# Last modulation block of the FFN summed on VectorE, four column blocks summed over half of the rows first, second norm from three means, three resident loads

## The chip, the cores and the metric

The program runs on one core of one Trainium2 chip. The metric is the device time of one execution in microseconds (us). Engines are named as in the profile: PE (TensorE, matrix products), DVE (VectorE), ACT (ScalarE), POOL (GpSimd) and SP (SyncE, which here issues the loads). SBUF is the on-chip memory, PSUM holds what PE writes (a PSUM tile is called a bank). "Landing" is the time from the issue of a load until its data is there.

## The reference, cut to what matters

A decoder layer on 256 rows of 2048 numbers. All numbers are float32.

```python
mod = silu(c) @ w_ada + b_ada                      # 2048 -> 6 x 2048
shift_a, scale_a, gate_a, shift_f, scale_f, gate_f = split(mod, 6)
h = rms_norm(x, g_attn_pre) * (1 + scale_a) + shift_a
proj = h @ w_in                                    # then attention of two kinds
mixed = concat([diff_out, dsa_out]) @ w_o
x = x + gate_a * rms_norm(mixed, g_attn_post)
h = rms_norm(x, g_ffn_pre) * (1 + scale_f) + shift_f
ff = (silu(h @ w_gate) * (h @ w_up)) @ w_down      # inner width 5632
x = x + gate_f * rms_norm(ff, g_ffn_post)
```

## The kernel before

**Tiles.** The 256 rows are two tiles t of 128 rows. The inner dimension of 2048 is 16 steps k of 128. A weight block of 4 k by 512 columns is 1 MB: `wload` (L159) loads it into `raw` (L163, a ring of six), and splits it into a high part `whi` (a copy on ACT, L179) and the rest `wlo` (a subtraction on DVE, L180), 1024 columns at a time, in rings of three. Each product of a k, a t and 512 columns is three matmuls (`mm3`, L192 high by high, L195 high by rest, L196 rest by high), so a block of 1 MB is 24 matmuls of 128x512.

**Stages.** `w_in` in groups of k; attention, mixed with the last group and with columns 0 to 1023 of `w_o`; columns 1024 to 2047 of `w_o` (two column blocks, ci = 2 and 3); the residual and the second norm; the transposed input of the FFN; the FFN in three groups of 4, 4 and 3 column blocks of 512, each gate, up and down.

**Modulation.** The vector `mod` is summed beside all this, in units of 1 MB of `w_ada` (L223), which share the ring of six. `ada_block` (L203) makes a unit either on PE, as four matmuls of 32x512 into the bank `ad` (L236; each shows as two rows of the trace), with an eviction at the end (L253), or on DVE, as four `scalar_tensor_tensor` of 128x512 into an accumulator `aacc` (L244). Shift and scale of the FFN (`modF`) are made in four blocks, 0 to 3, of 512 columns of each: 8 units, which are 64 rows of L236 on PE, or 32 instructions on DVE. When a block is summed, a few small matmuls and two DVE instructions put it into `modF`: L293 where it was on PE, L297 where it was on DVE. Block 2 is made on DVE (`F_DVE`, L41), the others on PE. Block b is needed for the steps k = 4b to 4b + 3 of the FFN's input. `side()` and the loops call `ada_step` to use some units after each weight block.

**Tail of `w_o`.** `tail_pair` (L786) runs the column blocks 2 and 3 for both t together, but keeps the last two weight blocks resident, and runs them first for t = 0, then for t = 1: 24 matmuls each, pinned in this order. After those of t = 0 comes `residual(0)`, which thus lies beside 24 matmuls of t = 1. The same function ends the program with `w_down`.

**Residual and second norm.** `post` (L773) squares a bank on ACT with a running sum (L783) and multiplies it by the gate on DVE (`y`, L784). `residual` (L852) sums the squares, takes the power −1/2 on POOL (`ry`, L156), adds y · ry to `x1` on DVE (two instructions, L859), squares the new x1 on ACT (two, L861), and on POOL adds (L862), scales (L155), takes the power (L156) and fills the diagonal matrix `dg[t]` (L864). The FFN's input `H2` is made by `h2_tiles` (L842): matmuls of x1 by `dg[t]` (L846, which transpose and norm), then shift and scale and the split into a high and a low half (`make_h`, L348, L350, L345, L347), first for k = 0 to 7, later for 8 to 15.

**First halves.** To start before blocks 2 and 3 of `modF` are there, the first `NSPLIT` column blocks of gate and up are summed over k = 0 to 7 and put aside in `part` (an ACT copy); the second half is added later on DVE (L925).

**Order.** A scheduler orders the instructions of all engines ahead of time; `keep_in_program_order` pins some. Each engine runs its queue in order, so an instruction that waits holds all behind it.

## Time and profile before

| | us |
|---|---|
| median of 3 runs (lowest to highest) | 1262.45 (1262.14 to 1264.23) |
| the profiled execution | 1263.92 |
| its span in the trace | 1262.1 |
| PE busy | 1230.5 (97%) |
| DVE busy | 763.6 (60%) |
| ACT busy | 573.1 (45%) |
| POOL busy | 23.2 (2%) |
| mean granted TensorE clock | 0.997 |

The span runs from the first to the last instruction of the trace; 1.8 us of the profiled execution lie outside it. A row of the timeline gives start, length, engine, source line, tiles (`out<-in`) and, in brackets, how long the engine was idle ahead of it and what released it. The lengths of matmuls overlap: one starts 0.2265 us after the other, though each is listed with 0.39. Rows with "x3" merge several instructions.

### The profile page before, as it was taken

The numbers are of one execution on the slowest core, as the hardware profiler recorded it, in microseconds if no ns is written. First come the engines' busy times: TensorE is split into PE (matmuls) and PEld (weight loads), VectorE is DVE, ScalarE is ACT, GpSimd is POOL, SyncE is SP. The second block draws the span as 40 slices with busy tenths as digits, with TensorE's granted clock in tenths as the row PEclk, the third lists the DMA queues.
The fourth block names the chain that finished last, engine by engine and source line by source line (L and its number), as shares of the span: only waits on it lengthen the run. The fifth ranks groups of instructions, "written<-read, shape, count | busy, mean of one in ns | idle before, by whom it ended". The sixth has DMA issues, their size and how long they took to land.

```text
span 1262.1 us, 15223 instructions
## 1 busy us (share of the span) xinstructions
PE 1230.5 (97%) x5912; PEld 948.6 (75%) x5912; DVE 763.6 (60%) x1155; ACT 573.1 (45%) x838; POOL 23.2 (2%) x63
## 2 busy tenths in 40 slices
...
GB/s 382 388 358 334 371 357 204 370 258 272 200 304 266 150 366 279 267 190 322 314 278 262 179 192 241 255 172 195 199 177 192 200 191 185 193 198 182 185 134 67
DMA packets 44713, 310.14 MB, mean 246 GB/s; under 512 B 5848, under 2 KB 5848, under 8 KB 7648
## 3 DMA queue, kind: packets, MB, share of 16 engines
...
q8 instruction: 46, 0.75, 0.2%
...
q10 hardware_dynamic: 272, 0.00, 0.0%
HBM read 307.05 MB, written 2.10 MB: 245 GB/s over the span
## 4 chain that ended last, share of the span: by engine, by line
PE 93%; DMA 2%; ACT 2%; DVE 1%; issue 1%; POOL 0%; SPq 0%; DVEq 0%; POOLq 0%
PE mm L195 27%; PE mm L192 27%; PE mm L196 27%; PE ad L236 5%; DMA raw<-in_w_ada_dram 1%; PE tr L490 1%; DMA raw<-in_w_in_dram 1%; PE tr L429 1%; PE tr L934 1%; PE tr L410 1%; PE tr L846 1%; PE tr L312 1%; DVE wlo L180 0%; PE tr L293 0%; PE tr L513 0%
## 5 line engine op out<-in xcount | busy, mean ns | idle before, releaser
L180 DVE TENSOR_TENSOR wlo<-raw,whi 128x1024 fp32r<-128x1024 f32 (+1 forms) x383 | 463.4, 1213 | 369.0 <-ACT whi L179 368.2
L179 ACT ACTIVATE whi<-raw 128x1024 fp32r<-128x1024 f32 (+1 forms) x383 | 401.0, 1051 | 519.5 <-PE mm L196 488.6
L195 PE MATMUL mm<-wlo,h 128*128 128x512 f32 (+1 forms) x1056 | 415.1, 393 | 0.8 <-DVE wlo L180 0.8
L196 PE MATMUL mm<-whi,h 128*128 128x512 f32 (+1 forms) x1056 | 410.9, 389 | 1.6 <-DVE h L350 1.6
L192 PE MATMUL mm<-whi,h 128*128 128x512 f32 (+1 forms) x1056 | 380.1, 393 | 1.9 <-ACT whi L179 1.0
L192 PEld LDWEIGHTS mm<-whi,h 128*128 128x128 f32 x1056 | 196.7, 188 | 63.3 <-issue 13.4
L195 PEld LDWEIGHTS mm<-wlo,h 128*128 128x128 f32 x1056 | 198.6, 188 | 60.3 <-issue 10.8
L196 PEld LDWEIGHTS mm<-whi,h 128*128 128x128 f32 x1056 | 198.6, 188 | 42.3 <-DVE h L350 2.1
L195 PE MATMUL mm<-wlo,gT 128*128 128x512 f32 x348 | 135.8, 390 | 0.0
L196 PE MATMUL mm<-whi,gT 128*128 128x512 f32 x348 | 135.4, 389 | 0.0
L192 PE MATMUL mm<-whi,gT 128*128 128x512 f32 x348 | 123.0, 390 | 0.0
L244 DVE SCALAR_TENSOR_TENSOR aacc<-raw,csil,aacc 128x512 f32<-128x512 f32 x126 | 94.0, 747 | 8.0 <-DMA raw<-in_w_ada_dram 5.3
L236 PE MATMUL ad<-raw,c 128*32 128x512 f32 (+2 forms) x640 | 82.8, 523 | 12.8 <-DMA raw<-in_w_ada_dram 12.8
L748 DVE TENSOR_TENSOR PR<-mm,PR 128x512 f32<-128x512 f32 (+1 forms) x88 | 57.0, 669 | 34.2 <-PE mm L196 34.0
L196 PEld LDWEIGHTS mm<-whi,gT 128*128 128x128 f32 x348 | 65.3, 188 | 13.9 <-issue 0.2
L195 PEld LDWEIGHTS mm<-wlo,gT 128*128 128x128 f32 x348 | 65.3, 188 | 13.6 <-issue 0.2
L192 PEld LDWEIGHTS mm<-whi,gT 128*128 128x128 f32 x348 | 65.3, 188 | 13.5
L195 PE MATMUL mm<-wlo,mixT 128*128 128x512 f32 x124 | 49.9, 402 | 0.0
L236 PEld LDWEIGHTS ad<-raw,c 128*32 128x32 f32 x640 | 17.9, 111 | 41.6 <-issue 26.7
L192 PE MATMUL mm<-whi,mixT 128*128 128x512 f32 x124 | 47.6, 402 | 0.7 <-ACT mixT L603 0.7
L196 PE MATMUL mm<-whi,mixT 128*128 128x512 f32 x124 | 45.9, 394 | 0.0
L195 PEld LDWEIGHTS mm<-wlo,mixT 128*128 128x128 f32 x124 | 23.3, 188 | 8.4 <-issue 1.7
(192 smaller groups left out, 673.2 us busy)
## 6 DMA issues: line engine op xcount, KB each, us to landing
...
```

Source lines behind the costliest of these rows:

```text
L179: made = [ACT.activation(hv, src, AF.Copy), DVE.tensor_tensor(lv, src, hv.bitcast(F32), op=ALU.subtract)]
L180: DVE.tensor_tensor(lv, src, hv.bitcast(F32), op=ALU.subtract)]
L192: i = PE.matmul(ps, lhsT=hi, rhs=whi, start=start, stop=False)
L195: PE.matmul(ps, lhsT=hi, rhs=wlo, start=False, stop=False)
L196: PE.matmul(ps, lhsT=lo, rhs=whi, start=False, stop=stop)
L236: PE.matmul(st["ps"][32 * j:32 * j + 32, :n], lhsT=c33[:, k, 1 - b:33 - b], rhs=w, start=(b == 0 and k < 4), stop=(b == nb - 1 and k >= 12 ...
L244: DVE.scalar_tensor_tensor(acc, w, csil[:, k:k + 1], acc, op0=ALU.mult, op1=ALU.add)
L312: PE.matmul(ps, lhsT=ones, rhs=accs[0], start=True, stop=True)
L410: PE.transpose(tr[:, i * P:(i + 1) * P], PR[:, t, c0:c0 + P], ident)
L429: PE.matmul(sc[i][:, SEG[t]], lhsT=st["q"][r, (2 * j + t) * P:(2 * j + t + 1) * P], rhs=ikT[r, :P * (t + 1)], start=True, stop=True)
L490: PE.matmul(sc[i][:, SEG[t]], lhsT=l, rhs=r, start=True, stop=True)
L748: DVE.tensor_tensor(dst, banks[c0][t][:, :n], dst, op=ALU.add)
```

## The change

- `F_DVE` is (2, 3): block 3 of `modF` is summed on DVE too. `FRATE` is 1: one unit instead of two after each half block of the first halves. `side()` in the tail stops two units into block 2 (`SIDE`).
- `NSPLIT` is 4: four column blocks are summed over k = 0 to 7 first. Their partial sums lie in `part`, in the buffer of `Ga` and in the tiles `xhi` and `xlo`. The load of `Gf` (the gate of the FFN), which shares the buffer of `Ga`, and its units come later, ahead of the fourth column block.
- `tail_pair` keeps the last three weight blocks resident: 36 pinned matmuls for each t. The first stays in the rings of `whi` and `wlo`, the second half in the rings and half in `xhi` and `xlo`, the third in the part of `H2` for k = 8 to 15, which is free then.
- The second norm doesn't square the new x1. With m1 the mean of the squared bank, m2 twice the mean of y · x1 and m3 the mean of y squared, ry = (m1 + eps)^(−1/2), and the mean square of the new x1 is m3 · ry² + m2 · ry + the mean square of x. `post_attn` makes the three sums by column block: two squares on ACT, y and a product with a running sum (`tensor_tensor_reduce`, L801) on DVE. `residual` then has a reduce, two small DVE steps, and three steps on POOL (`ry`, `r1`, `dg`); the updates of x1 come behind.
- `h2_tiles` works on pairs of k: shift and scale of one on DVE and of one on ACT, then one copy and one subtraction for both.

```diff
-F_DVE = (2,)
+F_DVE = (2, 3)
-FRATE = 2
+FRATE = 1
-NSPLIT = 2
+NSPLIT = 4
+SIDE = 2
...
     def tail_pair(rows, L, kbase, nk, cs, banks, side, done):
 
-        blocks = [(a, ci) for a in range(0, nk - 4, 4) for ci in cs]
-        for a, ci in blocks:
+        blocks = [(a, ci) for a in range(0, nk, 4) for ci in cs]
+        for a, ci in blocks[:-3]:
...
-        tl = {ci: wload(rows, kbase + nk - 4, 4, ci * 512, 512, ph2 if ci == cs[1] else None)
-              for ci in cs}
+
+        spare = [tuple(ph2.tile([P, 1024], F32R, tag=tag, name=nm(tag)) for tag in ("xhi", "xlo"))]
+        spare += [tuple(H2[:, i, k:k + 4, :].rearrange("p k q -> p (k q)") for i in range(2)) for k in (8, 12)]
+        homes = (None, (None, spare[0]), spare[1:])
+        tl = [(ci, wload(rows, kbase + a, 4, ci * 512, 512, homes[i])) for i, (a, ci) in enumerate(blocks[-3:])]
         for t in range(T):
-            for ci in cs:
-                for (k, _), (whi, wlo) in tl[ci].items():
+            for ci, ws in tl:
+                for (k, _), (whi, wlo) in ws.items():
...
     def side():
-        ada_step(1)
+        if used[0] < need_f1 + SIDE:
+            ada_step(1)
...
+    def post_attn(bank, t, ci):
+
+
+        cs_ = slice(ci * 512, ci * 512 + 512)
+        j = tr_bank()
+        ACT.activation(j, bank, AF.Square, scale=D ** -0.5, accum_out=st3[:, t, 0, ci:ci + 1])
+        DVE.tensor_tensor(y[:, t, cs_], bank, Ga[:, cs_], op=ALU.mult)
+        j2 = ph2.tile([P, 512], F32, tag="sil", name=nm("j2"), bufs=3)
+        DVE.tensor_tensor_reduce(out=j2, in0=y[:, t, cs_], in1=x1[:, t, cs_], scale=2.0 / D, scalar=0.0,
+                                 op0=ALU.mult, op1=ALU.add, accum_out=st3[:, t, 1, ci:ci + 1])
+        ACT.activation(j, y[:, t, cs_], AF.Square, scale=D ** -0.5, accum_out=st3[:, t, 2, ci:ci + 1])
...
     def residual(t):
+
         for ci in (2, 3):
-            post(banks[ci, t], t, ci, Ga, ssy, y)
-        DVE.tensor_reduce(sst[:, t:t + 1], ssy[:, t], axis=AX.X, op=ALU.add)
-        rstd(ry[:, t:t + 1], sst[:, t:t + 1], 1, D)
+            post_attn(banks[ci, t], t, ci)
+        DVE.tensor_reduce(mean[:, t], st3[:, t], axis=AX.X, op=ALU.add)
+        rt = ry[:, t:t + 1]
+        POOL.tensor_tensor(rt, mean[:, t, 0:1], nhalf[:, 0:1], op=ALU.pow)
+        m = mean[:, t, 1:2]
+        DVE.scalar_tensor_tensor(m, mean[:, t, 2:3], rt, m, op0=ALU.mult, op1=ALU.add)
+        tc.keep_in_program_order(
+            DVE.scalar_tensor_tensor(m, m, rt, msx[:, t:t + 1], op0=ALU.mult, op1=ALU.add))
+        POOL.tensor_tensor(r1[:, t:t + 1], m, nhalf[:, 0:1], op=ALU.pow)
+        POOL.tensor_scalar(dg[t], ident, r1[:, t:t + 1], None, op0=ALU.mult)
         for h in range(2):
             hs = slice(1024 * h, 1024 * h + 1024)
-            DVE.scalar_tensor_tensor(x1[:, t, hs], y[:, t, hs], ry[:, t:t + 1], x1[:, t, hs],
-                                     op0=ALU.mult, op1=ALU.add)
-            ACT.activation(y[:, t, hs], x1[:, t, hs], AF.Square, accum_out=ss1[:, t, h:h + 1])
-        POOL.tensor_tensor(sss[:, t:t + 1], ss1[:, t, 0:1], ss1[:, t, 1:2], op=ALU.add)
-        rstd(r1[:, t:t + 1], sss[:, t:t + 1], 1, D, POOL)
-        POOL.tensor_scalar(dg[t], ident, r1[:, t:t + 1], None, op0=ALU.mult)
+            tc.keep_in_program_order(
+                DVE.scalar_tensor_tensor(x1[:, t, hs], y[:, t, hs], rt, x1[:, t, hs], op0=ALU.mult, op1=ALU.add))
...
-    Gf = big.tile([P, D], F32, tag="Ga", name="Gf")
-    tc.keep_in_program_order(SP.dma_start(Gf, g_ffn_post[0].partition_broadcast(P)))
...
-            for b in range(4):
-                ada_gate(Gf, 5, b * 512, False)
         for lc in range(ng):
+            if fc == NSPLIT - 1:
+                Gf = big.tile([P, D], F32, tag="Ga", name="Gf")
+                tc.keep_in_program_order(SP.dma_start(Gf, g_ffn_post[0].partition_broadcast(P)))
+                for b in range(4):
+                    ada_gate(Gf, 5, b * 512, False)
```

The scheduler orders the changed program anew; up to the start of columns 1024 to 2047 of `w_o` (about 452 us of the trace) the order is as it was. Three places follow. Names carry the numbers of the program, so that `dg0` is of t = 0 and `dg1` of t = 1.

PE at the end of the tail, before: the last resident matmuls of t = 1, four units of block 3 (`ad826`), the transposes by `dg0`, and the first gate matmul.

```order
L195 MATMUL mm788_3876<-xlo837_4147,mixT286_1559 128x512
L196 MATMUL mm788_3876<-xhi836_4146,mixT287_1560 128x512
L236 MATMUL ad826_4123<-raw875_4366,c33_105 32x512 x4
L236 MATMUL ad826_4123<-raw876_4372,c33_105 32x512 x4
L236 MATMUL ad826_4123<-raw882_4412,c33_105 32x512 x4
L236 MATMUL ad826_4123<-raw883_4418,c33_105 32x512 x4
L846 MATMUL tr846_4236<-dg0_3871,x1_3850 128x128 x4
L846 MATMUL tr851_4257<-dg0_3871,x1_3850 128x128 x4
L192 MATMUL mm868_4326<-whi871_4330,h2_3866 128x512
```

The same place of PE in the changed program:

```order
L193 MATMUL mm791_3885<-h2_3876,mixT286_1564 128x512
L196 MATMUL mm791_3885<-h2_3876,mixT286_1564 128x512
L197 MATMUL mm791_3885<-h2_3876,mixT287_1565 128x512
L870 MATMUL tr836_4194<-dg0_3880,x1_3848 128x128 x4
L870 MATMUL tr839_4209<-dg0_3880,x1_3848 128x128 x4
L193 MATMUL mm850_4261<-whi853_4265,h2_3876 128x512
L196 MATMUL mm850_4261<-wlo854_4266,h2_3876 128x512
L197 MATMUL mm850_4261<-whi853_4265,h2_3876 128x512
L193 MATMUL mm850_4261<-whi853_4265,h2_3876 128x512
```

The units of block 3 are gone from PE, here and in the tail ahead; the transposes by `dg0` stand right behind the resident matmuls. Those by `dg1` stand behind 14 matmuls of `mm850`, and the third of these (L197) is the first that reads the low half of h2.

DVE at the residual of t = 0, before: the two `y` of t = 0, the sum and its scaling, the x1 updates, then the first `wlo` of the FFN and a `y` of t = 1.

```order
L784 TENSOR_TENSOR y_3853<-mm785_3873,Ga_142 128x512
L784 TENSOR_TENSOR y_3853<-mm787_3875,Ga_142 128x512
L855 TENSOR_REDUCE sst_3867<-ssy_3316 128x1
L155 TENSOR_SCALAR rs840_4181<-sst_3867 128x1
L859 SCALAR_TENSOR_TENSOR x1_3850<-y_3853,ry_3317,x1_3850 128x1024 x2
L180 TENSOR_TENSOR wlo872_4331<-raw870_4328,whi871_4330 128x1024
L784 TENSOR_TENSOR y_3853<-mm786_3874,Ga_142 128x512
```

The same place of DVE in the changed program, from the second `y` of t = 0; `raw872` is the last unit of block 2, `mm790` the last bank of t = 0:

```order
L245 SCALAR_TENSOR_TENSOR aacc871_4381<-raw872_4386,csil_103,aacc871_4381 128x512
L799 TENSOR_TENSOR y_3851<-mm790_3884,Ga_147 128x512
L245 SCALAR_TENSOR_TENSOR aacc871_4381<-raw872_4386,csil_103,aacc871_4381 128x512
L801 ISA j2831_4127,st3_119<-y_3851,x1_3848 128x512
L801 ISA st3_119 128x1
L181 TENSOR_TENSOR wlo854_4266<-raw852_4263,whi853_4265 128x1024
L890 TENSOR_REDUCE mean_3878<-st3_119 128x3
L181 TENSOR_TENSOR wlo856_4270<-raw852_4263,whi855_4269 128x1024
L894 SCALAR_TENSOR_TENSOR mean_3878<-mean_3878,ry_3321 128x1
L181 TENSOR_TENSOR wlo860_4306<-raw858_4303,whi859_4305 128x1024
L896 SCALAR_TENSOR_TENSOR mean_3878<-mean_3878,ry_3321,msx_117 128x1
L902 SCALAR_TENSOR_TENSOR x1_3848<-y_3851,ry_3321,x1_3848 128x1024 x2
```

Three `wlo` of the FFN's first blocks and the last sums of block 2 now stand in front of and between the steps of the residual. The first `y` of t = 0 and its product sum (L801) stand just ahead, each again between sums of `raw872`.

DVE in the first FFN blocks, before: `wlo`, and the shift, scale and split of h2.

```order
L180 TENSOR_TENSOR wlo888_4427<-raw886_4424,whi887_4426 128x1024
L348 TENSOR_SCALAR hf925_4672<-tr922_4659,modF_109 128x128
L350 TENSOR_TENSOR h2_3866<-hf924_4668,h2_3866 128x128
L350 TENSOR_TENSOR h2_3866<-hf925_4672,h2_3866 128x128
L180 TENSOR_TENSOR wlo890_4431<-raw886_4424,whi889_4430 128x1024
L348 TENSOR_SCALAR hf928_4685<-tr927_4680,modF_109 128x128
```

DVE at that stage of the changed program; `raw892` and `raw902` are units of block 3:

```order
L245 SCALAR_TENSOR_TENSOR aacc901_4561<-raw892_4510,csil_103,aacc901_4561 128x512
L181 TENSOR_TENSOR wlo877_4395<-raw873_4388,whi876_4394 128x1024
L245 SCALAR_TENSOR_TENSOR aacc901_4561<-raw892_4510,csil_103,aacc901_4561 128x512
L181 TENSOR_TENSOR wlo883_4435<-raw881_4432,whi882_4434 128x1024
L245 SCALAR_TENSOR_TENSOR aacc901_4561<-raw892_4510,csil_103,aacc901_4561 128x512 x2
L181 TENSOR_TENSOR wlo885_4439<-raw881_4432,whi884_4438 128x1024
L245 SCALAR_TENSOR_TENSOR aacc901_4561<-raw902_4566,csil_103,aacc901_4561 128x512 x2
L181 TENSOR_TENSOR wlo889_4475<-raw887_4472,whi888_4474 128x1024
L245 SCALAR_TENSOR_TENSOR aacc901_4561<-raw902_4566,csil_103,aacc901_4561 128x512
```

Between the `wlo` there are now the sums of block 3, four to each unit of 1 MB; where a unit's load is awaited, the next `wlo` waits behind it.

## Rows read from the trace of the kernel before

**Rows 1.** The page of the profile, part 1 (busy time, share of the span, instructions of each engine) and part 4 (the chain of work that ended last, by engine).

```profile
PE 1230.5 (97%) x5912; PEld 948.6 (75%) x5912; DVE 763.6 (60%) x1155; ACT 573.1 (45%) x838; POOL 23.2 (2%) x63
...
PE 93%; DMA 2%; ACT 2%; DVE 1%; issue 1%; POOL 0%; SPq 0%; DVEq 0%; POOLq 0%
```

**Rows 2.** Busy time in stretches of 20 us around the end of the attention part and in the FFN; columns: stretch, its length, busy us (and instructions) of PE, PEld, DVE, ACT and POOL, granted TensorE clock, share of the DMA engines, GB/s.

```profile
500.00:520.00 20.00, 16.13 (x95) 10.97 (x95) 13.90 (x25) 13.98 (x32) 5.42 (x11) 0.91 0.92 375
...
580.00:600.00 20.00, 20.00 (x94) 16.66 (x93) 19.51 (x25) 8.71 (x11) 0.00 (x0) 1.00 0.88 319
```

**Rows 3.** PE's instructions in order of time in the last part of `w_o`; columns: start us, us, engine, line, operation, tiles, number of instructions in the row.

```profile
463.06 0.39 PE L196 MATMUL mm<-whi,mixT 128*128 128x512 f32 x1
463.38 1.06 PE L236 MATMUL ad<-raw,c 128*32 128x512 f32 x8
...
464.71 0.39 PE L196 MATMUL mm<-whi,mixT 128*128 128x512 f32 x1
...
470.05 1.05 PE L236 MATMUL ad<-raw,c 128*32 128x512 f32 x2
...
490.40 1.06 PE L236 MATMUL ad<-raw,c 128*32 128x512 f32 x8
...
492.43 0.39 PE L196 MATMUL mm<-whi,mixT 128*128 128x512 f32 x1
492.75 1.07 PE L236 MATMUL ad<-raw,c 128*32 128x512 f32 x8
...
494.18 1.06 PE L236 MATMUL ad<-raw,c 128*32 128x512 f32 x6
...
495.51 0.39 PE L196 MATMUL mm<-whi,mixT 128*128 128x512 f32 x1
```

**Rows 4.** PE in order of time from the end of the tail into the first FFN block; same columns, and in brackets the idle time ahead of the row and what ended it.

```profile
497.78 0.39 PE L192 MATMUL mm<-whi,mixT 128*128 128x512 f32 x1
...
502.99 0.39 PE L196 MATMUL mm<-xhi,mixT 128*128 128x512 f32 x1
503.31 3.64 PE L236 MATMUL ad<-raw,c 128*32 128x512 f32 x32
508.25 2.05 PE L846 MATMUL tr<-dg,x 128*128 128x128 f32 x16 [1.30 <-POOL dg L864]
...
512.41 0.50 PE L196 MATMUL mm<-whi,h 128*128 128x512 f32 x1 [1.65 <-DVE h L350]
513.84 0.79 PE L192 MATMUL mm<-whi,h 128*128 128x512 f32 x1 [0.93 <-ACT h L345]
514.43 0.63 PE L195 MATMUL mm<-wlo,h 128*128 128x512 f32 x1
...
516.56 2.16 PE L846 MATMUL tr<-dg,x 128*128 128x128 f32 x16
```

**Rows 5.** DVE in order of time across the residual of the first 128 rows.

```profile
498.70 0.69 DVE L784 TENSOR_TENSOR y<-mm,Ga 128x512 f32<-128x512 f32 x1 [4.43 <-ACT tr L783]
499.30 0.15 DVE L855 TENSOR_REDUCE sst<-ssy 128x1 f32<-128x4 f32 x1
...
500.30 2.48 DVE L859 SCALAR_TENSOR_TENSOR x<-y,ry,x 128x1024 f32<-128x1024 f32 x2 [0.66 <-POOL ry L156]
...
504.44 2.35 DVE L180 TENSOR_TENSOR wlo<-raw,whi 128x1024 fp32r<-128x1024 f32 x2
```

**Rows 6.** POOL in order of time: two of the attention part, then the residuals of both halves of the rows.

```profile
256.88 0.70 POOL L156 TENSOR_TENSOR rsd<-rs,nhalf 128x2 f32<-128x2 f32 x1 [4.73 <-DVE rs L155]
...
270.87 1.12 POOL L156 TENSOR_TENSOR rsd<-rs,nhalf 128x2 f32<-128x2 f32 x1 [13.00 <-DVE rs L155]
...
505.80 1.04 POOL L155 TENSOR_SCALAR rs<-sss 128x1 f32<-128x1 f32 x1
506.92 0.56 POOL L156 TENSOR_TENSOR r<-rs,nhalf 128x1 f32<-128x1 f32 x1
507.58 0.62 POOL L864 TENSOR_SCALAR dg<-ident,r 128x128 f32<-128x128 f32 x1
...
513.26 0.19 POOL L155 TENSOR_SCALAR rs<-sss 128x1 f32<-128x1 f32 x1
```

**Rows 7.** DVE in order of time beside POOL's instruction at 270.87.

```profile
270.69 1.53 DVE L244 SCALAR_TENSOR_TENSOR aacc<-raw,csil,aacc 128x512 f32<-128x512 f32 x2
```

**Rows 8.** DVE's groups by line and shape over the whole span; columns: line, operation, tiles, shapes, number, busy us, mean ns of one, idle time ahead and what ended it.

```profile
L180 DVE TENSOR_TENSOR wlo<-raw,whi 128x1024 fp32r<-128x1024 f32 x374 | 456.5, 1224 | 365.4 <-ACT whi L179 364.7
L244 DVE SCALAR_TENSOR_TENSOR aacc<-raw,csil,aacc 128x512 f32<-128x512 f32 x126 | 94.0, 747 | 8.0 <-DMA raw<-in_w_ada_dram 5.3 <-DMA aacc<-in_b_ada_dram 1.6
...
L501 DVE CUSTOM_DVE_ANT_0 s<-tr,mask 128x256 f32<-128x256 f32 x16 | 6.7, 418 | 0.0
...
L501 DVE DVE_READ_ACCUMULATOR2_ANT mx<- 128x1 f32 x48 | 3.9, 82 | 0.0
```

**Rows 9.** From issue to landing of the 1 MB loads issued from 440 to 560 us: first those of `w_ada` (L223), then those of the weights (L163).

```profile
DMA to landing us min/median/max: 4.7/5.8/8.2
...
DMA to landing us min/median/max: 4.8/6.9/12.6
```

**Rows 10.** The last matmul of the program on PE, and DVE's sum of its result.

```profile
1252.63 0.39 PE L196 MATMUL mm<-xhi,gT 128*128 128x512 f32 x1
...
1253.39 0.68 DVE L780 TENSOR_TENSOR ff<-mm,ff 128x512 f32<-128x512 f32 x1
```

More of the change, by code (lines that the diff above doesn't have):

```diff
@@ L169, in wload @@
                 w = min(step, n - b)
-                if more is not None and a + m == nk:
-                    hi = more.tile([P, 1024], F32R, tag="xhi", name=nm("xhi"))
-                    lo = more.tile([P, 1024], F32R, tag="xlo", name=nm("xlo"))
+                home = more[a // 2] if more else None
+                if home is not None:
+                    hi, lo = home
                 else:
@@ L322, in layer @@
     rstd(rx, ssx, T, D)
+    msx = ct([P, T], "msx")
+    DVE.tensor_scalar(msx, ssx, 1.0 / D, EPS, op0=ALU.mult, op1=ALU.add)
+    st3 = ct([P, T, 3, 5], "st3")
+    POOL.memset(st3, 0.0)
+    POOL.memset(st3[:, :, 0, 4:5], EPS)
     def x_tiles(k0):
```

38 lines of the change are left out of this document (27 added, 11 removed).

## The prediction

> **What bounds the kernel now.** I read the page first. PE is busy 97% of the span and is 93% of the chain that ended last [rows 1]; the granted clock is 1.00 but for a few us. So a change pays only if it takes instructions off PE, or shortens one of PE's few waits. Next I read the timeline of PE where the change lies, from the last part of `w_o` into the first FFN block. Two things stand there. First, `ad` matmuls (L236), which sum block 3 of the FFN's shift and scale on PE: small clusters between the weight matmuls [rows 3], and 32 rows in a burst of 3.64 us [rows 4]. Second, the only waits of this region: 1.30 us for `dg`, 1.65 and 0.93 us for the first half of h2, and then a stretch at the low clock (mean 0.91 from 500 to 520 us [rows 2]). One weight matmul costs (502.99 − 497.78) / 23 = 0.2265 us at full clock [rows 4]; the five from 514.43 to 516.56 take 2.13 us where 1.13 would do, and the one at 513.84 takes 0.59 where some 0.3 would do, so the low clock cost 1.3 us. Waits and low clock together: 1.30 + 1.65 + 0.93 + 1.3 = 5.2 us.
>
> The profiled execution took 1263.92 us, 1.47 above the median; I sum against it and take 1.47 off at the end.
>
> **The `ad` matmuls go.** The cluster at 463.38 stands between matmuls that start at 463.06 and 464.71; two steps of 0.2265 would end at 463.51, so it costs 1.20 us [rows 3]. The two at 492.75 and 494.18 stretch the three steps from 492.43 (to 493.11) to 495.51: 2.40 us. With those at 470.05 and 490.40 at 1.2 each, the clusters cost 6.0 us; even the one of two rows at 470.05 lasts 1.05 us. The burst costs 3.64. Together **−9.64 us**. The finish of the blocks is even: block 2's eight L297 were spread out and block 3's L293 stood in one piece; now block 2's stand in one piece and block 3's are spread.
>
> **What takes their place.** Block 3 is 32 `scalar_tensor_tensor` on DVE, of 0.75 us each [rows 8], about 24 us, between the `wlo` of the first FFN blocks. Per 24 matmuls (5.44 us) DVE has there two `wlo`, 2.35 us [rows 5], and four of these: 5.3 us at most. That nearly fills it, but the kernel already has such a stretch: from 580 to 600 us DVE is busy 19.51 of 20.00 us, DMA moves 319 GB/s, and PE loses nothing [rows 2]. Price 0, while loads land in time (third rival). Two more column blocks in first halves mean eight more evictions on ACT and eight additions on DVE; the next blocks' matmuls cover them, and PE's matmuls stay the same in number. Without that cover an addition would hold a bank for its 0.69 us. The loads and DVE steps of `Gf` go some blocks later and are needed only at the end of the program. Price 0.
>
> **The residual, first 128 rows (t = 0).** Call E the end of the last matmul of `w_o` for t = 0. Behind it stand 24 matmuls of t = 1 in before (5.44 us), plus the burst; now 36, so 8.15 us. The chain to `dg0` loses both passes of ACT over x1 but gains DVE work queued in it, in the order shown above. `wlo826` is needed 24 matmuls ahead of E (E − 5.4); two sums and itself stand behind `wlo823` on DVE (1.4 + 1.2), so `wlo823` is ready by E − 8, and the load of `raw872` (block 2's last, ahead of the rows shown) takes the slot that it frees; at the median landing of 5.8 us [rows 9] it arrives at E − 2.2. Behind it queue four sums of block 2 (0.70 each back to back), two `y` (0.69), two product sums: L801 is the kind of L501, 0.42 at half its width [rows 8], so I take 0.69 of the same-sized `y` [rows 5] plus 0.08. That is 5.7 us: the last product sum ends at E + 3.5. Then `wlo854` (E + 4.7), the reduce of 0.15, `wlo856` (E + 6.1), the first mean step, `wlo860`, the second, the two x1 updates of 1.24 each.
>
> POOL's three steps lie beside these. In the trace POOL is held while DVE runs an instruction with both inputs in SBUF: L155 took 1.04 us at 505.80, beside two `wlo` that ended at 506.79, and 0.19 at 513.26 [rows 5, 6]; the power of two columns took 1.12 us at 270.87 beside two L244, and 0.70 otherwise [rows 6, 7]. (The Trainium skill, "SBUF — State Buffer", section "Who interferes with whom", states this as a lock: a DVE instruction with two SBUF inputs and a GpSimd instruction that reads SBUF exclude each other for the whole instruction. It speaks against this change, which sets POOL's steps beside such instructions; the trace agrees with the 1.04 us, and by the rule the sum is the one below.) So `ry` waits for the end of `wlo856` and is ready at E + 6.7; `wlo860` ends at E + 8.0, the second step at E + 8.1; `r1` waits for the first x1 update (E + 9.4), 0.56 [rows 6]; `dg0` for the second (E + 10.7), 0.62: E + 11.3. PE, done at E + 8.15, **waits 3.2 us**.
>
> **t = 1.** The transposes (L870) start at E + 11.4, take 1.8, and two matmuls follow; the third needs the low half of h2, which DVE makes behind two `y` and two product sums of t = 1: by the same durations at E + 15.1, so **a wait of 1.5**. Ten more matmuls end at E + 17.85. The chain of t = 1 meanwhile: reduce E + 14.7, `ry` E + 15.7, second step E + 16.25, `r1` and `dg1` again each behind an x1 update, E + 19.3: **a wait of 1.55**. Together 6.25, and with three such waits I count the low clock again, 1.3: 7.55 against 5.2, **+2.35 us**.
>
> **The end of the program.** With three resident blocks of `w_down` the first half's output leaves DVE earlier: now DVE takes up the last sum at 1253.39, though the last matmul ended at 1252.63 + 0.39 [rows 10]. **−0.3 us**.
>
> **Sum:** −9.64 + 2.35 − 0.3 = −7.6 us; 1263.92 − 7.6 = 1256.3, less 1.47: **1255 us**.
>
> **Rivals.** (1) *POOL is not held.* Then `ry`, `r1` and `dg` run beside DVE at 0.55 to 0.62 each: `dg0` at E + 8.8, `dg1` never late; only a wait of 0.7 and one of about 3 for h2 (its DVE queue stays) remain, 3.7 against 5.2. −9.64 − 1.5 − 0.3 = −11.4: 1251. For it: POOL needed only 0.56 and 0.62 us at 506.92 and 507.58 [rows 6], and it may slip in between two instructions of DVE. Against it: the 1.04 and 1.12 us.
>
> (2) *Block 2's sums hold the residual up.* `raw872` lands late, and `y`, the product sums and the `wlo` behind it in DVE's order all wait. At the longest landing of an ada load here, 8.2 us [rows 9], the chain is 2.4 longer: 1257.3. At 12.6, the longest of a weight load [rows 9]: 6.8 longer, 1261.7. The changed kernel does what it says on PE, but gives the gain back as a wait for `dg0`.
>
> (3) *Slower: block 3's loads set the pace of the first FFN blocks.* A slot of the ring that a unit's sums free takes a unit two further on, so a landing may last at most 2 × 5.44 − 4 × 0.70 = 8.1 us; beyond, DVE waits at a sum with the next `wlo` queued behind it, and PE follows at half the excess per block. Landings of 11.5 us on average would cost 1.7 us in each of eight blocks, 13.6 less the lead that DVE has built up (some 3 us): 1255 + 10.6 = 1265.6. For it: 5.44 us now move 2 MB, 385 GB/s, more than the 319 of [rows 2]; single loads took 12.6. Against it: the median is 5.8, and 375 GB/s were moved from 500 to 520 [rows 2].
>
> **How the numbers follow.** Forecast with POOL held 0.48, from 1252.5 to 1257; (1) 0.20; (2) 0.18, of it 0.05 above 1260; (3) 0.07; other small losses 0.07, more of them within 0.2% than not. 0.2% (2.5 us) is about what a measurement of this kernel can tell from no change. Faster by more, below 1259.9: 0.48 + 0.20 + 0.13 + 0.02 = 0.83; within 0.2%: 0.05 + 0.04 = 0.09; slower: 0.07 + 0.01 = 0.08. The range from 1250 to 1260 leaves out the best quarter of (1), the late part of (2) and (3): about 0.21.
>
> **What would show it.** Right: no `ad` rows on PE after 460 us, the last matmul of the tail 6 to 8 us earlier than 502.99; POOL rows of 1 us or more beside the x1 updates and `wlo`; three waits of PE, for `dg0`, h2 and `dg1`, of 6 us in all; no wait of PE for `wlo` from 520 to 580. (1) shows POOL rows of 0.55 to 0.62 and one wait of 3 us. (2) shows DVE idle for `raw` just before the first `y`. (3) shows PE waiting for `wlo`, and DVE for `raw<-in_w_ada_dram`, again and again in the first FFN blocks.

## The result, and the profile after

| us | before | changed |
|---|---|---|
| median of 5 runs each | 1264.23 | 1255.14 |
| lowest to highest | 1262.14 to 1264.90 | 1254.14 to 1255.38 |
| the profiled execution | 1263.92 | 1254.82 |
| its span | 1262.1 | 1253.0 |
| last matmul of the program starts at | 1252.63 | 1244.11 |

The ratio is 0.9930, 95% interval 0.9917 to 0.9944: faster by 9 us, well clear of the spread of the runs, though under 1%. The time is the predicted 1255, but the way there was not all as told, and one part of the agreement is chance: the first three of before's five runs, which were all there was when the forecast was made, had a median of 1262.45, all five have 1264.23. The forecast took 1.47 us off for a profiled run that, as it turned out, was no slower than usual. From profile to profile 7.6 us were forecast, and 9.1 came (1263.92 − 1254.82).

Lines have moved: `wlo` is L181 now, the sums on DVE L245, the transposes L870, the finish of a block made on DVE L298. First part 1 of the page of the changed kernel.

```profile
PE 1223.3 (98%) x5856; PEld 949.0 (76%) x5856; DVE 791.7 (63%) x1198; ACT 574.5 (46%) x837; POOL 25.5 (2%) x61
```

PE has lost 7.2 us of work, DVE has gained 28 ([rows 1]); PE still bounds the kernel. Next, PE in order of time across the end of the tail.

```profile
487.65 0.39 PE L197 MATMUL mm<-h,mixT 128*128 128x512 f32 x1
...
495.81 0.39 PE L197 MATMUL mm<-h,mixT 128*128 128x512 f32 x1
498.27 3.42 PE L870 MATMUL tr<-dg,x 128*128 128x128 f32 x16 [2.07 <-POOL dg L898]
501.43 0.80 PE L193 MATMUL mm<-whi,h 128*128 128x512 f32 x1
...
502.78 0.40 PE L193 MATMUL mm<-whi,h 128*128 128x512 f32 x1
...
506.46 2.05 PE L870 MATMUL tr<-dg,x 128*128 128x128 f32 x16 [1.00 <-POOL dg L898]
508.26 0.48 PE L197 MATMUL mm<-whi,h 128*128 128x512 f32 x1
...
509.05 0.40 PE L197 MATMUL mm<-whi,h 128*128 128x512 f32 x1
509.28 1.84 PE L298 MATMUL tr<-ones,aacc 128*128 128x1 f32 x16
510.99 0.47 PE L193 MATMUL mm<-whi,h 128*128 128x512 f32 x1
```

Compare with [rows 4]. The tail's last matmul starts 7.18 us earlier (495.81 against 502.99) and nothing stands between it and the transposes but a wait of 2.07 us. So E, the end of the last matmul of t = 0, is 487.65 + 0.39 = 488.04. The transposes by `dg0` took 501.43 − 498.27 = 3.16 us, those by `dg1` 508.26 − 506.46 = 1.80. Cut into short stretches, the columns being those of [rows 2] for PE alone, the trace says why.

```profile
496.00:498.30 2.30, 0.23 (x2) 1.00 0.66 278
498.30:501.40 3.10, 3.10 (x16) 0.56 0.02 5
501.40:503.20 1.80, 1.80 (x7) 0.81 0.00 0
503.20:505.00 1.80, 1.80 (x9) 1.00 0.00 0
```

The granted clock (the column behind PE's count) was 1.00 while PE waited, fell to 0.56 under the transposes, mostly the lower level of 1.2 GHz, and was back at 1.00 from 503.2. Then DVE across the residual of t = 0.

```profile
485.91 0.75 DVE L245 SCALAR_TENSOR_TENSOR aacc<-raw,csil,aacc 128x512 f32<-128x512 f32 x1 [2.00 <-DMA raw<-in_w_ada_dram]
486.58 0.68 DVE L799 TENSOR_TENSOR y<-mm,Ga 128x512 f32<-128x512 f32 x1
...
490.38 0.68 DVE L801 CUSTOM_DVE_ANT_0 j<-y,x 128x512 f32<-128x512 f32 x1
...
490.99 1.22 DVE L181 TENSOR_TENSOR wlo<-raw,whi 128x1024 fp32r<-128x1024 f32 x1
...
492.21 1.21 DVE L181 TENSOR_TENSOR wlo<-raw,whi 128x1024 fp32r<-128x1024 f32 x1
493.86 0.22 DVE L894 SCALAR_TENSOR_TENSOR mean<-mean,ry 128x1 f32<-128x1 f32 x1 [0.44 <-POOL ry L892]
...
495.13 0.21 DVE L896 SCALAR_TENSOR_TENSOR mean<-mean,ry,msx 128x1 f32<-128x1 f32 x1
495.26 2.47 DVE L902 SCALAR_TENSOR_TENSOR x<-y,ry,x 128x1024 f32<-128x1024 f32 x2
```

It is the chain of the prediction, step for step: DVE waits for `raw872`, then sums, `y` and product sums take turns until 491.07, then `wlo` stand around the steps of the norm. And POOL:

```profile
492.36 1.46 POOL L892 TENSOR_TENSOR ry<-mean,nhalf 128x1 f32<-128x1 f32 x1 [80.74 <-DVE mean L890]
495.42 1.53 POOL L897 TENSOR_TENSOR r<-mean,nhalf 128x1 f32<-128x1 f32 x1 [1.60 <-DVE mean L896]
497.05 1.17 POOL L898 TENSOR_SCALAR dg<-ident,r 128x128 f32<-128x128 f32 x1
...
503.61 1.52 POOL L897 TENSOR_TENSOR r<-mean,nhalf 128x1 f32<-128x1 f32 x1 [0.80 <-DVE mean L896]
```

Steps of 0.56 and 0.62 us [rows 6] take 1.46 to 1.53 and 1.17 beside `wlo` and the x1 updates. `ry` at 492.36 ends at 493.82, when the `wlo` of 492.21 has ended; `r1` and `dg` end behind one x1 update each. The windows of the first FFN blocks, with the columns of [rows 2]:

```profile
520.00:540.00 20.00, 20.00 (x90) 16.57 (x89) 18.55 (x22) 10.80 (x13) 0.00 (x0) 1.00 0.97 372
540.00:560.00 20.00, 20.00 (x102) 16.92 (x101) 16.85 (x23) 10.48 (x14) 0.00 (x0) 1.00 0.95 354
```

PE has no idle time from 520 to 560 us (nor from there to 580), with DVE at 18.55 of 20.00 us and 372 GB/s moved: block 3's sums cost PE nothing. Last, the end of the program (PE, then DVE), against [rows 10].

```profile
1244.11 0.39 PE L197 MATMUL mm<-h,gT 128*128 128x512 f32 x1
...
1244.53 0.69 DVE L787 TENSOR_TENSOR ff<-mm,ff 128x512 f32<-128x512 f32 x1 [1.29 <-PE mm L197]
```

DVE takes up the last sum 0.03 us behind the end of the last matmul (1244.11 + 0.39); before it was 0.37 behind. What lies behind the start of the last matmul has shrunk from 1262.1 − 1252.63 = 9.47 to 1253.0 − 1244.11 = 8.89 us.

### The profile page after: what moved, and what is told of

The parts are those of the page before. It is cut to its first block, busy times and chain, and to the rows that moved or that the text cites. A ratio compares the mean times of both kernels' runs of the same rounds, so it can differ in the third digit from the quotient of the medians.

```text
span 1253.0 us, 15155 instructions
## 1 busy us (share of the span) xinstructions
PE 1223.3 (98%) x5856; PEld 949.0 (76%) x5856; DVE 791.7 (63%) x1198; ACT 574.5 (46%) x837; POOL 25.5 (2%) x61
## 4 chain that ended last, share of the span: by engine, by line
PE 58%; issue 1%; DVE 0%; ACT 0%; DVEq 0%; POOLq 0%; POOL 0%
PE mm L196 19%; PE mm L197 19%; PE mm L193 19%; PE tr L983 1%; PE tr L870 0%; PE tr L313 0%; PE tr L298 0%; DVE ff L1021 0%; ACT tr L790 0%; DVE ff L787 0%; DVEq L1057 0%; POOLq L1057 0%; POOL ry L157 0%; DVE sst L1030 0%; DVE rs L156 0%
## 5 line engine op out<-in xcount | busy, mean ns | idle before, releaser
L181 DVE TENSOR_TENSOR wlo<-raw,whi 128x1024 fp32r<-128x1024 f32 (+1 forms) x379 | 458.0, 1213 | 320.4 <-ACT whi L180 319.8
L180 ACT ACTIVATE whi<-raw 128x1024 fp32r<-128x1024 f32 (+1 forms) x379 | 396.7, 1050 | 501.7 <-PE mm L197 460.8
L197 PE MATMUL mm<-whi,h 128*128 128x512 f32 (+1 forms) x1056 | 410.2, 388 | 0.0
L196 PEld LDWEIGHTS mm<-wlo,h 128*128 128x128 f32 x1056 | 198.5, 188 | 59.9 <-issue 11.4
L197 PEld LDWEIGHTS mm<-whi,h 128*128 128x128 f32 x1056 | 198.4, 188 | 40.3 <-issue 1.3
L196 PE MATMUL mm<-wlo,gT 128*128 128x512 f32 x340 | 132.7, 390 | 0.0
L197 PE MATMUL mm<-whi,gT 128*128 128x512 f32 x340 | 132.3, 389 | 0.0
L245 DVE SCALAR_TENSOR_TENSOR aacc<-raw,csil,aacc 128x512 f32<-128x512 f32 x156 | 116.4, 747 | 23.0 <-DMA raw<-in_w_ada_dram 18.6
L193 PE MATMUL mm<-whi,gT 128*128 128x512 f32 x340 | 120.0, 390 | 0.0
L237 PE MATMUL ad<-raw,c 128*32 128x512 f32 (+2 forms) x576 | 74.7, 522 | 11.6 <-DMA raw<-in_w_ada_dram 11.6
L197 PEld LDWEIGHTS mm<-whi,gT 128*128 128x128 f32 x340 | 63.8, 188 | 13.5 <-issue 0.2
L193 PEld LDWEIGHTS mm<-whi,gT 128*128 128x128 f32 x340 | 63.8, 188 | 13.2
L196 PE MATMUL mm<-wlo,mixT 128*128 128x512 f32 x116 | 46.1, 397 | 0.2 <-DVE wlo L181 0.2
L193 PE MATMUL mm<-whi,mixT 128*128 128x512 f32 x116 | 44.3, 400 | 0.7 <-ACT mixT L611 0.7
L197 PE MATMUL mm<-whi,mixT 128*128 128x512 f32 x116 | 42.7, 393 | 0.0
L193 PEld LDWEIGHTS mm<-whi,mixT 128*128 128x128 f32 x116 | 21.6, 188 | 6.7 <-ACT mixT L611 0.9
```

Of the source, the lines that this page charges most:

```text
L180: made = [ACT.activation(hv, src, AF.Copy), DVE.tensor_tensor(lv, src, hv.bitcast(F32), op=ALU.subtract)]
L181: DVE.tensor_tensor(lv, src, hv.bitcast(F32), op=ALU.subtract)]
L193: i = PE.matmul(ps, lhsT=hi, rhs=whi, start=start, stop=False)
L196: PE.matmul(ps, lhsT=hi, rhs=wlo, start=False, stop=False)
L197: PE.matmul(ps, lhsT=lo, rhs=whi, start=False, stop=stop)
L237: PE.matmul(st["ps"][32 * j:32 * j + 32, :n], lhsT=c33[:, k, 1 - b:33 - b], rhs=w, start=(b == 0 and k < 4), stop=(b == nb - 1 and k >= 12 ...
```

## The experiments

The theory: the gain is the `ad` matmuls that leave PE, and the other parts only keep it from being given back as a wait for `dg`. The rivals: the new norm or the third resident block gains by itself, or the sums would do it alone. All kernels compute the same function. Each was timed in turns with the kernel before (1263.85, 1264.31 and 1263.83 us in the three groups), and ratios are to it. The diffs are against the changed kernel, unless the text says otherwise.

### Block 3 back on PE, the rest kept

```diff
-F_DVE = (2, 3)
+F_DVE = (2,)
```

> The changed kernel with block 3 of modF made on PE again; all else as changed. Theory (the gain is the ad matmuls that left PE, 1.2 us for each place where they stand between weight matmuls): the order has one unit ahead of the transposes by dg0, where PE waits anyway, and some twelve other places, of which ten split units in the first FFN blocks. 12 x 1.1 = 13 us, less 0.7 for the finish: about 1267 us, no better than before. Rival (the ad matmuls stood in waits, and the gain is the residual with its three means and its longer cover): up to 4 us above the changed kernel, 1255 to 1259.

Measured: 1267.18 us, ratio 1.0028 (1.0017 to 1.0039), slower than before. Without the move of the sums all else of the change gains nothing, and the move of the sums is worth 12 us under it. These 12 are not the 9.64 of the kernel before: the changed order breaks block 3 into more places. PE in order of time shows the clusters, now in the first FFN blocks:

```profile
524.53 0.39 PE L197 MATMUL mm<-whi,h 128*128 128x512 f32 x1
524.85 1.06 PE L237 MATMUL ad<-raw,c 128*32 128x512 f32 x6
...
526.50 1.04 PE L237 MATMUL ad<-raw,c 128*32 128x512 f32 x2
527.47 0.50 PE L196 MATMUL mm<-wlo,h 128*128 128x512 f32 x1
```

Three steps of 0.2265 should take 0.68 us from 524.53; they take 2.94, so each cluster costs 1.13 us, the one of two rows as much as that of six. The 1.2 of the prediction [rows 3] holds, and the price hangs on the number of places (13 here; five and a burst in [rows 3, 4]), not of rows. One of the 13, at 496.74, lay in PE's wait: the transposes start 2.60 us behind the start of the tail's last matmul (499.02 − 496.42), where the changed kernel's start 2.46 behind (498.27 − 495.81). The other twelve make 13.6 us. Against the changed kernel's trace the tail ends 0.6 later, and the transposes and the matmuls behind them, at a granted clock of 1.00, take 1.7 less: so up to the finish of block 2 (510.68 against 509.28), with two clusters, this trace is 1.4 us later. By the program's last matmul it is 12.50 later (1256.61 against 1244.11), and ten clusters lie between, 11.3 us at 1.13 each. The medians differ by 12.0.

### The sums alone, on the kernel before

Against the kernel before:

```diff
-F_DVE = (2,)
+F_DVE = (2, 3)
```

> The kernel before with block 3 of modF on DVE, and nothing else of the change. Theory (the sums pay only if they find room on DVE): PE loses 9.6 us of ad matmuls, but thirteen sums of 0.7 us now stand on DVE between the steps of the residual, which has 5.4 us of cover; dg0 comes 6 to 10 us later, so 1258 to 1263. Rival (taking the sums off PE is the whole gain, wherever DVE makes them): 1254 to 1256, like the changed kernel.

Measured: 1264.86 us (11 runs), 1.0008 (1.0000 to 1.0017): no gain at all, less than even the theory had left of it. PE has lost the same `ad` matmuls, and its trace gives nearly all of them back at the transposes. PE in order of time, and the window of [rows 2]:

```profile
505.98 3.78 PE L846 MATMUL tr<-dg,x 128*128 128x128 f32 x16 [8.27 <-POOL dg L864]
```

```profile
500.00:520.00 20.00, 12.47 (x63) 10.27 (x63) 18.84 (x37) 10.20 (x25) 5.39 (x9) 0.74 0.86 308
```

The wait for `dg0` has grown from 1.30 to 8.27 us, and the clock fell behind it, so that the transposes took 3.44 instead of 1.80 (the next matmul starts at 509.42). That is 6.97 + 1.64 = 8.6 of the 9.64 us, and `dg1` is waited for too, 0.97. The burst of [rows 4] had been cover for the residual as well as work: 3.64 of the 6.97 are the burst that is gone, and 3.3 a longer residual, whose `y` and x1 updates stand behind block sums and `wlo` in DVE's queue.

### Two resident blocks instead of three

```diff
-        for a, ci in blocks[:-3]:
+        for a, ci in blocks[:-2]:
...
-        homes = (None, (None, spare[0]), spare[1:])
-        tl = [... for i, (a, ci) in enumerate(blocks[-3:])]
+        homes = (None, (None, spare[0]))
+        tl = [... for i, (a, ci) in enumerate(blocks[-2:])]
```

> The changed kernel with two resident weight blocks in both tails instead of three, so 24 matmuls of t = 1 behind those of t = 0 instead of 36. Theory (PE waits for dg0 because the chain is longer than its cover): 2.7 us less cover, the wait grows from 2.1 to some 4.8 us, and the end of the program loses some 0.5: 1258 us. Rival (the chain hangs on the late load of block 2's last unit, not on the cover): within 1 us of the changed kernel, 1255 to 1256.

Measured: 1260.09 us, 0.9972 (0.9961 to 0.9983): 5 us of the gain gone, more than both theories gave. PE in order of time:

```profile
502.28 3.78 PE L870 MATMUL tr<-dg,x 128*128 128x128 f32 x16 [6.00 <-POOL dg L898]
```

The wait is 3.93 us longer than in the changed kernel; the cover is shorter by 12 matmuls, 2.72 us, and the residual itself came 1.2 us later (in this order a `y` and a product sum of t = 1 stand between its steps on DVE). The transposes took 0.36 more, and the end of the program (the same function serves `w_down`) 0.6: together 4.9, of 5.4 us between the two spans and 4.95 between the medians. Against the sums alone (1264.86) this kernel is 4.8 us faster, with the same cover. That is the worth of the parts that are not the third block (the order of the units, four column blocks in halves, the new norm, h2 by pairs), and no run divides it among all of them.

### The old second norm

```diff
-            post_attn(banks[ci, t], t, ci)
...
+            post(banks[ci, t], t, ci, Ga, ssy, y)
...
```

The rest of the edit puts back the sum, `ry`, the x1 updates, the squares of x1 on ACT and POOL's steps behind them, in place of the three means.

> The changed kernel with the residual of before: x1 is updated, squared on ACT, and POOL has five steps; no product sums on DVE. Theory (the three means take ACT's squares off the chain but put two product sums of 0.77 us on it, and POOL stays held): dg0 some 10.2 us after the last matmul of t = 0, as with three means (10.4), and dg1 no later: within 1.5 us of the changed kernel, 1254 to 1256.5. Rival (the three means are what shortened the chain): dg0 and dg1 2 us later each, 1258 to 1260.

Measured: 1256.24 us (1253.98 to 1258.77), 0.9942 (0.9930 to 0.9955). The interval overlaps that of the changed kernel: the three means bought nothing that these runs can tell. POOL and PE in order of time:

```profile
495.89 0.55 POOL L157 TENSOR_TENSOR r<-rs,nhalf 128x1 f32<-128x1 f32 x1
496.54 0.61 POOL L901 TENSOR_SCALAR dg<-ident,r 128x128 f32<-128x128 f32 x1
...
497.21 3.56 PE L872 MATMUL tr<-dg,x 128*128 128x128 f32 x16 [1.96 <-POOL dg L901]
502.23 0.50 PE L193 MATMUL mm<-whi,h 128*128 128x512 f32 x1 [1.46 <-ACT h L885]
```

The old chain has two passes of ACT more, but its `r1` and `dg` fall beside two `y`, which read one input from PSUM, and take 0.55 and 0.61. By these rows the new norm, which saves the passes of ACT, pays for it with two product sums of 0.68 in DVE's queue and with POOL's held steps: the wait is 1.96 us in the one and 2.07 in the other. For t = 1 this trace has no wait for `dg1`, and one of 1.46 for h2.

### `dg` made on ACT

```diff
-        POOL.tensor_scalar(dg[t], ident, r1[:, t:t + 1], None, op0=ALU.mult)
+        ACT.activation(dg[t], ident, AF.Copy, scale=r1[:, t:t + 1])
```

> The changed kernel with dg[t] filled on ACT instead of POOL; the order of all other instructions is the same. Theory (POOL is held until DVE's second x1 update ends): dg comes 0.3 us after r1 instead of 1.2, the waits for dg0 (2.1) and dg1 (1.0) shrink by 0.9 each: 1253.3 us, if the low clock stays as it is. Rival (PE would wait for x1 or for h2 anyway): within 0.5 us of the changed kernel, 1255.

Measured: 1253.72 us, 0.9918 (0.9905 to 0.9932), 1.4 us below the changed kernel's 1255.14, which is of another group of runs, with intervals that overlap. `dg` takes 0.40 us on ACT and the wait for `dg1` is gone; the one for `dg0` was 2.21 in this trace, because DVE had waited 3.20 us for `raw872` there, 1.2 longer than in the changed kernel.

### POOL's steps ahead of the x1 updates: two attempts

Rival (1) asks what POOL takes when it isn't held. To have `r1` and `dg` run before DVE starts on x1, the updates read a copy of `ry` that POOL makes. At first the copy's place was left to the scheduler:

```diff
+        rt2 = ct([P, 1], f"rt2_{t}")
+        POOL.tensor_copy(rt2, rt)
...
-                DVE.scalar_tensor_tensor(x1[:, t, hs], y[:, t, hs], rt, ...
+                DVE.scalar_tensor_tensor(x1[:, t, hs], y[:, t, hs], rt2, ...
```

> The changed kernel with the x1 updates made to wait for a copy of ry that POOL makes behind dg, so that DVE runs no instruction with two inputs in SBUF beside r1 and dg. Theory (POOL is held by DVE's instructions with two inputs in SBUF): r1 takes 0.55 us instead of 1.53 and dg 0.62 instead of 1.17, while ry, still beside wlo, keeps its 1.46; x1 comes 1.7 us later, so the transposes start as before and the time is that of the changed kernel, 1254.5 to 1256. Rival (POOL's steps are slow by themselves): r1 and dg keep 1.5 and 1.2, and the transposes come 3 us later: 1258 or more.

Measured: 1256.37 us, 0.9937 (0.9923 to 0.9950). The scheduler put the copy ahead of `r1`, the x1 updates ran beside `r1` and `dg` as ever (1.53 and 1.17 us), and the run tells nothing on the question. With POOL's order pinned as `ry`, `r1`, `dg`, copy:

```diff
+        tc.keep_in_program_order(POOL.tensor_tensor(r1[:, t:t + 1], m, nhalf[:, 0:1], op=ALU.pow))
+        tc.keep_in_program_order(POOL.tensor_scalar(dg[t], ident, r1[:, t:t + 1], None, op0=ALU.mult))
+        rt2 = ct([P, 1], f"rt2_{t}")
+        tc.keep_in_program_order(POOL.tensor_copy(rt2, rt))
```

> The changed kernel with POOL's order pinned to ry, r1, dg and then a copy of ry, for which the x1 updates wait. In pool_alone the copy had moved ahead of r1 and r1 was beside the updates again, so that run told nothing. Now y of t = 1 (one input in PSUM, one in SBUF) stands beside r1. Theory (POOL is held only by DVE's instructions with two inputs in SBUF): r1 takes 0.55 us instead of 1.53, dg 0.6 to 1.2, for a product sum starts beside it, and ry beside wlo keeps its 1.46; x1 is updated some 1.8 us later, so the transposes come no earlier: 1254.5 to 1257. Rival (POOL's steps are slow by themselves): r1 keeps 1.5 us, and the transposes come 3 us later: 1258 or more.

Measured: 1255.04 us, 0.9929 (0.9916 to 0.9942), the time of the changed kernel. POOL, and DVE beside it, in order of time:

```profile
494.94 0.68 DVE L799 TENSOR_TENSOR y<-mm,Ga 128x512 f32<-128x512 f32 x1
495.10 0.55 POOL L897 TENSOR_TENSOR r<-mean,nhalf 128x1 f32<-128x1 f32 x1 [1.60 <-PE mm L197]
495.65 0.69 DVE L801 CUSTOM_DVE_ANT_0 j<-y,x 128x512 f32<-128x512 f32 x1
495.75 1.08 POOL L898 TENSOR_SCALAR dg<-ident,r 128x128 f32<-128x128 f32 x1
...
496.99 1.28 DVE L904 SCALAR_TENSOR_TENSOR x<-y,rt,x 128x1024 f32<-128x1024 f32 x1 [0.64 <-POOL rt L900]
```

`r1` beside a `y` takes 0.55 us, where it took 1.53 beside an x1 update; `dg`, beside a product sum with both inputs in SBUF that ended at 496.34, takes 1.08 instead of 0.61. So POOL was held, by DVE's instructions with two SBUF inputs. It buys no time here: the transposes need x1 as well, and the first x1 update now ends at 498.27 (PE waited 3.28 us). Removing the hold only moved the end of the chain to DVE.

### The last sums of block 2 out of the tail

```diff
-SIDE = 2
+SIDE = 6
```

> The changed kernel with four more of block 2's units used inside the tail of w_o (six instead of two). In this order no sum of block 2 stands ahead of the steps of the residual of t = 0. Theory (DVE's wait of 2.0 us for the last unit of block 2, and its four sums, hold the chain to dg0): the chain is 2 us shorter or more, the wait for dg0 goes from 2.1 to under 0.5 us, that for dg1 stays: 1253 us, and 1251.5 if the low clock goes with the wait. Rival (the chain is bounded by the steps themselves, wlo and POOL): within 0.7 us of the changed kernel.

Measured: 1253.44 us (1253.27 to 1253.79), 0.9914 (0.9900 to 0.9927); the interval overlaps the changed kernel's. No sum of block 2 is left in the residual's DVE queue, and DVE doesn't wait for `raw` in the tail, but the wait for `dg0` is 1.44 us, where the theory had under 0.5: the `wlo` and POOL's held steps still stand in the chain. PE:

```profile
497.71 2.05 PE L870 MATMUL tr<-dg,x 128*128 128x128 f32 x16 [1.44 <-POOL dg L898]
...
505.34 2.05 PE L870 MATMUL tr<-dg,x 128*128 128x128 f32 x16 [0.98 <-POOL dg L898]
```

With both edits, `SIDE = 6` and `dg` on ACT:

> Both: six units of block 2 in the tail, and dg[t] filled on ACT. Theory: the gains add where they touch different waits; no wait for dg0, 0.1 us for dg1: 1251 us, 1250 without the low clock. Rival: the time is that of the better one of the two, 1253.

Measured: 1252.92 us (1251.72 to 1253.10), 0.9907 (0.9894 to 0.9921). The wait for `dg0` is down to 0.61 us, followed by 0.54 for ACT, and there is none for `dg1`:

```profile
497.91 1.16 PE L870 MATMUL tr<-dg,x 128*128 128x128 f32 x8 [0.61 <-ACT dg L898]
499.61 1.16 PE L870 MATMUL tr<-dg,x 128*128 128x128 f32 x8 [0.54 <-ACT tr L803]
```

### Two column blocks in halves instead of four

```diff
-FRATE = 1
+FRATE = 2
...
-NSPLIT = 4
+NSPLIT = 2
```

> The changed kernel with two column blocks in first halves instead of four, and so two units instead of one after each half block. Theory (DVE has room for one unit beside 24 matmuls, 2.35 + 2.8 us of 5.44, not for two, 2.35 + 5.6): DVE falls behind in the eight half blocks by 2.5 us each, less the lead and the rings of three, and PE waits for wlo or for the last block of modF: 1259 to 1263. Rival (the number of first halves doesn't matter): 1254.5 to 1256.

Measured: 1256.14 us (6 runs, 1254.81 to 1261.21), 0.9946 (0.9930 to 0.9962). The theory of this run, that DVE would fall behind by 2.5 us in each half block, was mostly wrong: the profiled execution has one such wait, and its windows show why it was no worse.

```profile
534.02 0.73 PE L193 MATMUL mm<-whi,h 128*128 128x512 f32 x2 [1.55 <-ACT whi L180]
```

```profile
520.00:540.00 20.00, 18.45 (x91) 15.29 (x90) 19.64 (x29) 8.61 (x12) 0.00 (x0) 1.00 0.97 382
540.00:560.00 20.00, 20.00 (x105) 16.90 (x104) 14.77 (x22) 10.82 (x17) 0.99 (x2) 1.00 0.97 401
```

The `whi` of that row waited for a weight load, and the load's issue had waited 4.0 us for DVE's sums to free its slot. DVE is full (19.64 of 20.00 us) for one stretch only; in the next it has 5 us to spare. The median is 1.0 us above the changed kernel's in the first group of runs and 1.15 above its repeat below; the intervals overlap. One run took 1261.21, so the margin of `NSPLIT = 2` is thin. Four blocks are worth about 1 us, if anything.

### The changed kernel and the best one, side by side

> The changed kernel as it is, beside the next one on the same chip: 1255 us, ratio 0.993.

> The kernel of side6_dg_act once more, beside the changed kernel. Theory (the two waits for dg were worth 2 to 3 us): 2 to 3 us below the changed kernel in the same stretch of runs. Rival (the difference of 2.2 us was that of two chips or two hours): within 1 us of it.

Measured on one chip: the changed kernel 1254.99 us (1254.45 to 1256.72), 0.9931 (0.9919 to 0.9943); with `SIDE = 6` and `dg` on ACT 1252.48 (1251.61 to 1253.28), 0.9909 (0.9896 to 0.9922). The second is 2.5 us faster, no run of the one reaching a run of the other, and so faster than the kernel before and the changed one. From 440 us on PE waits 4.08 us in the repeat's trace (0.81 for a `wlo`, 1.44 and 1.00 for `dg`, 0.83 for h2) and 1.41 in the other's (0.61 for `dg0`, 0.55 for ACT, 0.25 for h2): 2.67 of the 2.90 us by which its last matmul starts earlier (1240.84 against 1243.74). The repeat of the changed kernel also shows how the waits change while the time stays. Its transposes:

```profile
498.47 2.05 PE L870 MATMUL tr<-dg,x 128*128 128x128 f32 x16 [1.44 <-POOL dg L898]
501.07 0.50 PE L193 MATMUL mm<-whi,h 128*128 128x512 f32 x1 [0.55 <-ACT h L883]
```

And POOL's `ry` of t = 0, with the `wlo` beside it on DVE:

```profile
492.88 0.55 POOL L892 TENSOR_TENSOR ry<-mean,nhalf 128x1 f32<-128x1 f32 x1 [81.01 <-DVE mean L890]
492.92 1.23 DVE L181 TENSOR_TENSOR wlo<-raw,whi 128x1024 fp32r<-128x1024 f32 x1
```

Here the clock didn't fall, the transposes took 2.05 in the listing, and waits for h2 appear that the slow transposes of the first trace had hidden; a wait of 0.8 for a `wlo` ahead of E makes up the rest. And `ry`, which took 1.46 us in the first trace, where the `wlo` had started 0.15 us ahead of it, took 0.55 here, where it started 0.04 us ahead of the `wlo`. The execution took 1254.45 us, the first one 1254.82.

## Why the prediction came out right, step by step

**The `ad` matmuls: right.** −6.0 us of clusters and −3.64 of burst were forecast. The start of the tail's last matmul moved by −7.18 us: the clusters, and some 1.8 us for the spread L297 of block 2, against 0.3 us that the kernel was late already at 442 us, and a wait of 0.21 for a `wlo`. The burst is gone from behind it. Putting the work back, in more places, cost 12 us, at 1.13 for each cluster. This is shown.

**The finish of the blocks is even: wrong by 0.9 us.** Block 2's finish now stands in one piece and takes 510.99 − 509.05 − 0.23 = 1.71 us. Block 3's L293 before had started at 521.11, between matmuls at 520.88 and 521.92, and cost 0.81. The two forms aren't the same work: L293 is four small matmuls (8 rows), L298 eight (16 rows). The step took them as equal. The spread L297 of block 2 cost 1.8 us before, by the same subtraction at its five places; that block 3's spread L298 cost as much now is an estimate.

**Block 3 on DVE at no cost: right.** No wait for `wlo` from 520 to 580 us, DVE at 18.55 of 20.00 at the most, and even with half of the room (`NSPLIT = 2`) one wait of 1.55. Rival (3) didn't come: DVE's longest wait for a `raw` of block 3 was 0.98 us.

**The residual of t = 0: the chain right, a little too long.** From E the trace gives, forecast in brackets: `raw872` usable at −2.1 (−2.2), last product sum +3.0 (+3.5), `ry` +5.8 (+6.7), second step +7.3 (+8.1), `r1` +8.9 (+10.0), `dg0` +10.2 (+11.3). Each step has the forecast's order and releaser. Half of the excess came in the sums, `y` and product sums, which I put at 5.7 us and which took 5.2 (485.91 to 491.07); the rest came by tenths at each step. PE waited 2.07 us instead of 3.2.

**That wait is cover against chain,** and the same subtraction reads the runs. Cover is PE's work of t = 1 behind E; the chain is cover plus the wait that the trace shows.

| kernel | cover, us | wait for `dg0` | chain |
|---|---|---|---|
| before | 5.44 + 3.64 | 1.30 | 10.4 |
| sums alone | 5.44 | 8.27 | 13.7 |
| two resident | 5.44 | 6.00 | 11.4 |
| changed | 8.15 | 2.07 | 10.2 |
| changed, the repeat | 8.15 | 1.44 | 9.6 |
| old norm | 8.15 | 1.96 | 10.1 |
| `SIDE = 6` | 8.15 | 1.44 | 9.6 |
| and `dg` on ACT | 8.15 | 0.61 | 8.8 |

So the change as a whole leaves the chain as long as it was, and it is the third block that pays for the lost burst. One and the same program had 10.2 in one trace and 9.6 in the other, so `SIDE = 6` alone, with 9.6, isn't shown to shorten the chain. With `dg` on ACT as well it is 8.8, in that trace and in the one of the repeat (wait 0.61 in both), and that kernel has the best time.

**POOL is held: right, with a condition that the prediction left out.** `ry` and `r1` of t = 0 took 1.46 and 1.53 us in the changed kernel, and a step took 0.55 beside a DVE instruction that reads PSUM. Rival (1) is out. (The Trainium skill, "SBUF — State Buffer", section "Who interferes with whom", says that a DVE instruction with two SBUF inputs contends with a GpSimd instruction that reads SBUF; the 0.55 beside `y` and the 1.53 beside the x1 update agree.) The condition is that DVE's instruction has started first: in the repeat `ry` started 0.04 us ahead of the `wlo` and took 0.55, 0.9 less than in the first trace; with `SIDE = 6` it started 0.17 ahead and took 0.55 too. The price of rival (1) was too high, though: pinning POOL's steps ahead brought 0, since x1 is needed too.

**t = 1 and the low clock: the sum too large, and differently made.** Forecast: 3.2 + 1.5 + 1.55 of waits and 1.3 of low clock, 7.55 us against 5.2 before. Measured: 2.07 + 0 + 1.00 of waits; at the low clock 3.16 − 1.80 = 1.36 us on the transposes, and three matmuls from 501.43 to 502.78 that cost 1.35 where 0.68 would do, 0.67. Together 5.1 us: −0.1 instead of the +2.35 on record. So of the signs, the three waits of 6 us in all did not come: there were two, of 3.07. That the wait for h2 was there in the chain, with the slow transposes lying over it, is inferred from the repeat, where they ran at full clock and waits for h2 of 0.55 and 0.28 appear. This is the term that was mis-sized, by 2.45 us. (Its text counts "ten more matmuls" ahead of the transposes by `dg1`; its time, E + 17.85, is that of twelve, which the order of 14 asks for.)

**The end of the program:** −0.58 us, −0.3 forecast.

**The sum.** −7.6 forecast from profile to profile; +0.9 for the finish, −2.45 for the residual, −0.3 for the end, +0.2 for the `wlo` ahead of E and +0.3 for the start give −8.9 of the −9.1 that came. The median of 1255 was met because these 1.5 us and the 1.47 that I took off for the choice of run cancel. Rival (2) didn't decide either: `raw872` was there at E − 2.1 in the profiled run, where the forecast had it, and at E − 2.6 in the repeat, and the 2.00 us that DVE waited for it were part of the forecast's chain. Its mechanism is real but small: with `dg` on ACT `raw872` came at E − 1.2, and the wait for `dg0` was 2.21 us in spite of the faster step.

**What stays open:** whether the three means are worth up to 1 us or nothing (1256.24 against 1255.14, with runs 5 us apart), and the same for four column blocks in halves. Both would want many more runs. The making of h2 by pairs of k was not run by itself, nor do the runs say how the 4.8 us between the sums alone and two resident blocks divide. Why the clock fell behind some waits and not behind others stays open too.
